# One attention layer on one core: start loads by block, forget gates by log of sigmoid, an earlier gate evacuation, and a last row tile in 512, 256, 256

## The chip, the core and the metric

The kernel runs on one core of a Trainium2 chip. The core has five engines that run beside each other and wait for each other by semaphores: TensorE (PE in the profile; its weight loads are PEld), VectorE (DVE), ScalarE (ACT), GpSimd (POOL) and SyncE (SP), which here only issues DMAs. The metric is the time of one execution on the device, in microseconds (us).

## What is computed

One layer on x of 1024 rows by 1024 columns, in fp32. A normalised and modulated input u feeds one wide projection; sixteen heads of width 64 attend over it, eight by forgetting attention (FoX) and eight by stick-breaking; an output projection and a second LayerNorm follow.

```python
mod = silu(c) @ w_ada + b_ada                       # shift, scale, gate
u = layer_norm(x) * (1.0 + scale) + shift
h = u @ w_in                                        # fq fk fv fg ff sq sk sv sg
log_f = log_sigmoid(ff + b_f)                       # 8 forget gates a row
f_cum = cumsum(log_f, axis=1)
# FoX:  softmax(q k / 8 + f_cum[q] - f_cum[k], causal) @ v
# stick-breaking:  exp(log_sigmoid(z) + sum of later log_sigmoid(-z)) @ v
y = concat(y_fox * silu(fg), y_sb * silu(sg)) @ w_out
out = layer_norm(2 ** 0.25 * x + gate * y) * ln_g + ln_b
```

## The kernel before, in words

Every fp32 operand of a matmul is split into a high part, rounded to the matmul's format, and a low part, the remainder; a product is three matmuls (high by high, low by high, high by low) into one PSUM tile. A u block is 128 of the 1024 columns of u, transposed; its parts are `uh` and `ul`, its number is kb, 0 to 7.

**The start (lines 627 to 747).** While rows 0 to 511 of u are made, block by block, five projections (START, line 570: q, k and the gate of pair 0, q and k of pair 1) are accumulated from each block as it appears. For a block kb:

- SyncE loads its modulation weights (`load_ss`, `wss`, 1 MB) and its projection weights (`load_w4`, `raws`, 256 KB for four projections; the fifth projection has two loads of its own, `load_w1`, each for four blocks). SyncE's queue is in program order, and it is written out by hand. `wss` has three buffers, so the load of block kb+3 waits until block kb's reductions are done.
- VectorE makes scale and shift with two reductions (`mod_part`, line 230, which ends with a short read into `modc`).
- TensorE transposes the block of x into the one PSUM tile `xT_early` (`u_turn`), ScalarE writes `uh` and the full value (`u_round`, lines 248 and 249, in the tile `xT_early`), and VectorE writes the remainder `ul` (`u_rest`, line 261).
- ScalarE rounds the block's weights and GpSimd makes their remainder (`start_split`, lines 608 and 609; tiles `whi_stk`, `hw` and, for the fifth projection, `whi_sth`).
- TensorE multiplies (`start_steps`, lines 622 and 625).

Step kb of the loop at line 682 multiplies block kb and prepares block kb+1. In the kernel before, the split of block 4 is issued at step 3 together with block 5's, behind block 4's rounding; blocks 4 and 5, and 6 and 7, come with one load of 512 KB each; and the two `wss` of blocks 6 and 7 come whole.

**The passage to rows 512 to 1023 (lines 736 to 838).** Row tiles 4 to 7 of x are loaded last. VectorE makes their statistics (lines 197, 198 and 189), GpSimd the inverse deviation (lines 191, 192 and 211), and ScalarE (tiles 4 and 5) or VectorE (6 and 7, line 217) normalises. Meanwhile TensorE makes v for rows 0 to 511 (`v_first`, lines 354 to 356), with a copy by ScalarE and a remainder by VectorE for each half of a tile (lines 362 and 363). Then `late_round(kb)` transposes and rounds block kb for rows 512 to 1023. PSUM tiles named T have two buffers: the tile `v_0_1` of the second `v_first` has one, the late block 0 the other, and late block 1 takes the buffer of `v_0_1` once VectorE has read it for the last time. The tiles named acc have two buffers as well: `st_g0b`, the gate of pair 0 for rows 512 to 1023, takes the buffer of `st_g0`, which `evac_g` (lines 289 and 290: tanh on ScalarE, then a multiply on VectorE) has to release.

**The forget gates (`gen_forget`, line 383)** run once, beside the stick-breaking units of pairs 2 and 3, when fillers reach them. With a = |ff|, log sigmoid is min(ff, 0) - ln(1 + exp(-a)): ScalarE does Exp and then Ln, each with a function table that has to be loaded first, and goes back to Sigmoid for the attention.

**The end (`o_half`, line 921).** Row tiles of 128 rows run through the output projection in 512-column groups, and each group adds the residual (line 934) and takes statistics (line 935). The last row tile has three groups, 512, 320 and 192 columns, 24 matmuls each. When its last group is done, the mean and inverse deviation follow, then `(r - mean) * ln_g` for each group (line 942), then the scaling and `ln_b`: by VectorE for 512 and 192 columns (line 946), by ScalarE and GpSimd for 320 (lines 958 and 959), and three DMAs write the row tile.

The order of instructions on TensorE and SyncE in the start is that of the program; on the other engines a list scheduler chooses it, within `after(...)`, which puts an instruction behind another.

Of the kernel before, what the change touches and what calls it, by code (L numbers as in the profile page):

```python
# [27 lines left out]
def tile_hybrid_layer(  # L28
# [122 lines left out]

    def load_ss(kb):
        t = sb.tile([P, 2, D], F32, tag="v", bufs=3, name=f"wss_{kb}")
        for a in ((0, 1), (1, 2)) if kb < 6 else ((0, 2),):
            nc.sync.dma_start(t[:, a[0]:a[1], :], w_ss[kb, :, a[0]:a[1], :])
        wss_sb.append(t)

    bss_sb = cp.tile([P, NB, 2], F32, tag="bss", name="bss_sb")
# [127 lines left out]

    def evac_g(p, ch, acc, sg):
        s = slice(ch * 512, ch * 512 + 512)
        nc.scalar.activation(sg[:, s], acc, AF.Tanh, scale=0.5)
        nc.vector.scalar_tensor_tensor(sg[:, s], sg[:, s], 1.0, acc, op0=ALU.add, op1=ALU.mult)  # L290

    def m_step(acc, tiles, kt, ch):
        hi, lo = tiles[kt // 4]
# [19 lines left out]
    def evac_m(p, m, ch, acc, heads=(0, 1)):  # L313
        if m == 0:
            evac_q(p, ch, acc, qst[p], heads)
        elif m == 1:
            return evac_k(p, ch, acc, kst[p], klo[p], heads)
        else:
            evac_g(p, ch, acc, sgt[p])

    def gen_m(p, m):
        tiles = fetch_m(p, m)
# [60 lines left out]
    def gen_forget():  # L383
        ff = fsb.rearrange("p h t -> p (h t)")
        ab = cp.tile([P, 64], F32, tag="fab", name="fab")
        lf = flf[:, 1:]
        nc.vector.scalar_tensor_tensor(ab, ff, -1.0, ff, op0=ALU.mult, op1=ALU.max)
        nc.scalar.activation(ab, ab, AF.Exp, scale=-1.0)
        nc.scalar.activation(ab, ab, AF.Ln, bias=1.0)
        for _ in range(FLOG):  # L390
            yield
        with after(*lows):
            nc.vector.scalar_tensor_tensor(lf, ff, 0.0, ab, op0=ALU.min, op1=ALU.subtract)

        pre = ff
        nc.vector.tensor_tensor_scan(pre, flf[:, 0:64], later.rearrange("p h t -> p (h t)"), initial=0.0,
                                     op0=ALU.add, op1=ALU.mult)
        for _ in range(FROW):
            yield
        scratch = att_tile("fscratch")  # L400
        tri, fr = scratch[:, :P], scratch[:64, P:2 * P]
        nc.gpsimd.memset(tri, 1.0)
        nc.gpsimd.affine_select(out=tri, in_=tri, pattern=[[1, P]], base=0,
                                channel_multiplier=-1, compare_op=ALU.is_ge, fill=0.0)
        fp = t_tile("fcum")[:, :64]
        nc.tensor.matmul(fp, tri, lf, start=True, stop=False)
        nc.tensor.matmul(fp, ones.to_broadcast([P, P]), pre, start=False, stop=True)
        fc = cp.tile([P, 64], F32, tag="fab", name="fc")
        nc.scalar.activation(fc, fp, AF.Copy, scale=-1.0)
        yield  # L410
        yield
        ft = t_tile("frow")[:64, :P]
        nc.tensor.transpose(ft, fc, ident)
        nc.scalar.copy(fr, ft)
        nc.sync.dma_start(f_dr.rearrange("h (t p) -> (h t) p", p=P), fr)
        yield
# [174 lines left out]
    def load_w1(h, raw=None):  # L591
        raw = start_raw(1) if raw is None else raw
        nc.sync.dma_start(raw, w_qkg[START[NW][0], START[NW][1], h])
        raw_w["h", h] = raw.rearrange("p (m c) -> p m c", m=4)
# [40 lines left out]
    load_w4(2)  # L635
    load_ss(3)
    load_w4(3)
    load_w1(1)
    for t in range(4):
        norm_stats(t)  # L640
        if t:
# [13 lines left out]
    with after(rounded):  # L655
        start_split(("k", 1))
    load_ss(4)
    load_w4(4, 2)
    for p in range(2):
        make_q(p)  # L660
        make_k(p)
# [20 lines left out]
    for kb in range(NB):  # L682
        last = kb == NB - 1
        if last:
            start_steps(ALL[:2], acc0, kb)
            for n in range(2):
                evac_m(*START[n], 0, acc0[n])
            start_steps(ALL[2:], acc0, kb)
            break
        start_steps(ALL[:4], acc0, kb, parts=(0,))  # L690
        if kb == 0:
            u_turn(2, tp=xt_early)
        elif kb > 1:
            u_turn(kb + 1, tp=xt_early)
        with after(*split_at["k", kb + 1][:1] if kb < 2 else ()):
            rounded = u_split(kb + 1) if kb == 0 else u_round(kb + 1)
        if kb == 0:
            with after(rounded):
                start_split(("h", 0))
            mod_terms(2)  # L700
        else:
            parts = range(2 if kb + 2 < NB else 0)
            late = kb in (3, 4)
            mod_terms(kb + 2, () if late else parts[:1])
            rest = in_turn(u_rest, kb + 1)
            mod_terms(kb + 2, parts if late else parts[1:])
        if kb == 0:
            start_steps(ALL[:4], acc0, kb, parts=(1,))
        elif kb == 1:
            start_steps(ALL[:4], acc0, kb, parts=(1,))  # L710
            for k in range(2):
                start_steps(ALL[4:], acc0, k)
        else:
            start_steps(ALL[4:], acc0, kb, parts=(0,))
            start_steps(ALL, acc0, kb, parts=(1,))
        if kb == 2:
            start_split(("h", 1))
        elif kb < 2:
            start_split(("k", kb + 2))
        elif kb + 2 < NB:  # L720
            with after(rounded):
                for k in ((4, 5) if kb == 3 else (kb + 2,)):
                    start_split(("k", k))
        if kb + 5 < NB:
            load_ss(kb + 5)
            if kb == 0:
                load_w4(6, 2)
        if kb == 2:
            for n in range(2):
                v0_load(n)  # L730
            load_x(4)
            for n in range(2, 4):
                v0_load(n)
            for t in range(5, NB):
                load_x(t)
        if kb == 5:
            with after(*split_at["k", NB - 1]):
                for n in range(4):
                    v0_split(n)
            norm_stats(4)  # L740
            norm_stats(5)
            norm_x(4)
        if kb == 6:
            with after(rest):
                for t in (6, 7):
                    norm_stats(t)
            make_v(0)
# [57 lines left out]
        load_gate(kt)  # L805
    v_first(2, late_acc[:, 1, :])
    with after(*late_round(0)):
        evac_m(*START[2], 0, acc0[2])
    rounded = late_round(1)
    v_first(3, acc_tile("v_0_3"))  # L810

    acc1 = [late_acc[:, 0, :], late_acc[:, 1, :], acc_tile("st_g0b")]
# [86 lines left out]
    OUT_ORDER = (6, 7, 4, 5, 2, 3, 0, 1)  # L899

    def groups(t):
        return ((0, 512), (512, 832), (832, 1024)) if t == OUT_ORDER[-1] else ((0, 512), (512, 1024))

    def o_step(t, h, pr):
        if pr == 0:
# [15 lines left out]
    def o_half(t, h):  # L921
        ts_ = slice(t * P, (t + 1) * P)
        s = slice(*groups(t)[h])
        ng = len(groups(t))
        if h == 0:
            xr = big("k", 4, f"xr_{t}")
            nc.sync.dma_start(xr, x[ts_, :])
            res[t] = (att_tile(f"r_{t}"), xr, sb.tile([P, 3, 6], F32, tag="st", bufs=3, name=f"st_b{t}")[:, :ng, :])
        r, xr, st = res[t]
        last = t == OUT_ORDER[-1]  # L930

        acc = o_acc[t, h][:, :s.stop - s.start]
        to = acc if last else r[:, s]
        nc.vector.scalar_tensor_tensor(to, xr[:, s], ALPHA, acc, op0=ALU.mult, op1=ALU.add)
        nc.vector.bn_stats(st[:, h, :], to)
        if h == ng - 1:
            mv, rs = ln_finish(st, f"b{t}")
            cuts = [slice(*g) for g in groups(t)]
            mid = [o_acc[t, j][:, :c.stop - c.start] if last else r[:, c] for j, c in enumerate(cuts)]

            def first(j):
                nc.vector.scalar_tensor_tensor(mid[j], mid[j], mv[:, 0:1], lgb[0][:, 0, cuts[j]],
                                               op0=ALU.subtract, op1=ALU.mult)

            def second(j):
                nc.vector.scalar_tensor_tensor(r[:, cuts[j]], mid[j], rs[:, 0:1], lgb[0][:, 1, cuts[j]],
                                               op0=ALU.mult, op1=ALU.add)
                (nc.scalar if j == 2 else nc.sync).dma_start(out[ts_, cuts[j]], r[:, cuts[j]])

            if not last:  # L950
                for j in range(2):
                    first(j)
                    second(j)
                return
            for j in (1, 0, 2):
                first(j)
            c = cuts[1]
            nc.scalar.activation(r[:, c], mid[1], AF.Copy, scale=rs[:, 0:1])
            nc.gpsimd.tensor_tensor(r[:, c], r[:, c], lgb[0][:, 1, c], op=ALU.add)
            nc.sync.dma_start(out[ts_, c], r[:, c])  # L960
            for j in (0, 2):
                second(j)

    def gen_out_first(t):
        for h in range(2):
# [203 lines left out]
```

## Time and profile before

| what | value |
|---|---|
| median of 3 runs | 683.64 us (683.54 to 684.12) |
| the profiled execution | 684.15 us, its span 682.44 us |
| granted TensorE clock | 0.998 |
| TensorE busy | 671.7 us (98%), 3713 matmuls |
| VectorE, ScalarE, GpSimd busy | 485.0, 380.7, 404.9 us |
| DMA, mean over the span | 119 GB/s |

The span runs from the first to the last instruction of one profiled execution; the rest of that execution's time, 1.7 us, lies around it. In the rows of a timeline stand the start in us from the span's start, the duration in us, the engine, the line, the operation, the tiles written and read, the shape, how many neighbours were merged, and in brackets how long the engine had been idle and what released it. Ends of matmuls are modelled, so for TensorE the distance between starts says more than the durations.

### The profile page before, as it was taken

To read this page: it belongs to the slowest core of one execution; us is meant where nothing else is said; L and a number is where in the kernel's file an instruction comes from. 1 tells how busy PE (TensorE), PEld (TensorE's weight loads), DVE (VectorE), ACT (ScalarE), POOL (GpSimd) and SP (SyncE) were. 2 spreads that over 40 slices of the span, in tenths; PEclk is the share of its full clock that TensorE was granted. 3 is DMA by queue.
4 is the path that set the end of the run, shared out by engine and by line. 5 is a ranking of instruction groups with operands and counts; after the bars stand their busy time and mean duration, and the time that the engine had idled before them with its cause. 6 is when DMAs were issued, how large, how long until landed. Compare 5 with 4: busy or idle time off the path is not lost.

```text
span 682.4 us, 11191 instructions
## 1 busy us (share of the span) xinstructions
PE 671.7 (98%) x3713; PEld 572.5 (84%) x3713; DVE 485.0 (71%) x996; ACT 380.7 (56%) x857; POOL 404.9 (59%) x529
## 2 busy tenths in 40 slices
PE   8999999999999999999999999999999999999995
PEld 5788898888997888889988888889988888888885
DVE  6696779868666777777676675766676777875645
ACT  5567377756567666666665564656565766521000
POOL 5550179756447656566369778786785365655411
PEclk9999999999999999999999999999999999999999
DMA  9973422112102122122034455363352297153301
GB/s 327 408 271 143 147 74 79 30 37 60 32 10 70 41 54 56 39 54 55 27 114 144 147 162 155 109 182 127 118 172 64 65 343 309 58 179 103 119 32 61
DMA packets 45272, 81.54 MB, mean 119 GB/s; under 512 B 5216, under 2 KB 19360, under 8 KB 44960
## 3 DMA queue, kind: packets, MB, share of 16 engines
q1 hardware_dynamic: 43632, 76.54, 34.4%
q10 hardware_dynamic: 1584, 4.31, 1.9%
q8 instruction: 29, 0.48, 0.3%
q14 instruction: 27, 0.22, 0.1%
HBM read 60.34 MB, written 16.29 MB: 112 GB/s over the span
## 4 chain that ended last, share of the span: by engine, by line
PE 95%; ACT 2%; DVE 2%; POOL 1%; issue 0%; DVEq 0%; POOLq 0%
PE m L296 10%; PE m L297 10%; PE m L298 10%; PE pv L530 10%; PE T L513 9%; PE S L462 5%; PE S L461 5%; PE o L917 4%; PE o L916 4%; PE o L915 4%; PE v L354 4%; PE v L356 4%; PE v L355 4%; PE st_q L622 1%; PE st_late L622 1%; PE st_k L622 1%
## 5 line engine op out<-in xcount | busy, mean ns | idle before, releaser
L516 DVE TENSOR_TENSOR pt<-T,pt 128x512 fp32r<-128x512 f32 (+2 forms) x192 | 102.6, 553 | 43.5 <-ACT pt L515 41.9
L515 ACT CAST pt<-T 128x512 fp32r<-128x512 f32 (+2 forms) x192 | 88.6, 478 | 64.5 <-PE T L513 62.6
L296 PE MATMUL m<-uh,whi 128*128 128x512 f32 x304 | 123.5, 406 | 0.0
L298 PE MATMUL m<-uh,wlo 128*128 128x512 f32 x304 | 119.9, 394 | 0.0
L297 PE MATMUL m<-ul,whi 128*128 128x512 f32 x304 | 119.8, 394 | 0.0
L496 POOL TENSOR_TENSOR be<-be,kp 128x127 f32<-128x127 f32 (+3 forms) x64 | 78.9, 1233 | 37.8 <-DVE kp L494 26.2
L490 DVE TENSOR_TENSOR_SCAN kp<-kp,floor 128x512 f32<-128x512 f32 (+2 forms) x64 | 65.0, 1016 | 25.5 <-ACT kp L483 24.2
L530 PE MATMUL pv<-pt,v 128*128 128x512 f32 x320 | 82.9, 389 | 0.0
L477 POOL TENSOR_SCALAR a<-a,l 128x1024 f32<-128x1024 f32 (+3 forms) x64 | 48.3, 754 | 36.0 <-DVE l L475 25.3
L461 PE MATMUL S<-k,q 128*128 128x512 f32 (+5 forms) x192 | 68.9, 360 | 0.3 <-ACT be L485 0.3
L298 PEld LDWEIGHTS m<-uh,wlo 128*128 128x128 f32 x304 | 57.2, 188 | 13.6
L474 ACT ACTIVATE a<-a,nm 128x1024 f32<-128x1024 f32 (+3 forms) x64 | 49.8, 778 | 29.2 <-DVE nm L469 28.9
L296 PEld LDWEIGHTS m<-uh,whi 128*128 128x128 f32 x304 | 57.3, 188 | 10.0 <-PE T L513 0.3
L462 PE MATMUL S<-kl,qz 128*128 128x512 f32 (+5 forms) x192 | 65.4, 342 | 0.0
L297 PEld LDWEIGHTS m<-ul,whi 128*128 128x128 f32 x304 | 57.4, 189 | 9.0
L530 PEld LDWEIGHTS pv<-pt,v 128*128 128x128 f32 x320 | 55.5, 189 | 9.0
L546 POOL TENSOR_TENSOR ty<-ty,sg 64x256 f32<-64x256 f32 x64 | 46.9, 732 | 23.9 <-issue 10.9
L469 DVE CUSTOM_DVE_ANT_0 a<-S,fb 128x1024 f32<-128x1024 f32 (+3 forms) x64 | 48.2, 754 | 16.6 <-PE S L462 11.7
L435 ACT CAST qz<-q 64x128 fp32r<-64x128 f32 x128 | 37.3, 296 | 33.6 <-PE S L462 32.4
L354 PE MATMUL v<-whi_v,uh 128*128 128x256 f32 (+1 forms) x192 | 54.8, 285 | 0.0
L356 PE MATMUL v<-wlo_v,uh 128*128 128x256 f32 (+1 forms) x192 | 54.3, 283 | 0.0
L483 ACT ACTIVATE kp<-S 128x128 f32<-128x128 f32 (+3 forms) x64 | 42.0, 657 | 21.8 <-PE S L462 20.5
(290 smaller groups left out, 1624.6 us busy)
## 6 DMA issues: line engine op xcount, KB each, us to landing
raw<-in_w_qkg_dram SPq DMA_DIRECT2D x38, 256.0 KB, 2.7
wss<-in_w_ss_dram SPq DMA_DIRECT2D x12, 512.0 KB, 8.6
x<-in_x_dram SPq DMA_DIRECT2D x8, 512.0 KB, 7.3
k<-k SPq DMA_DIRECT2D x32, 128.0 KB, 2.3
wg<-in_w_gate_dram SPq DMA_DIRECT2D x8, 512.0 KB, 4.5
raw_o<-in_w_out_dram SPq DMA_DIRECT2D x16, 256.0 KB, 3.0
fb<-f_dr ACTq DMA_DIRECT2D x8, 512.0 KB, 4.4
wo_dr<-whi_o SPq DMA_DIRECT2D x16, 256.0 KB, 2.0
```

The costliest lines, as they stand in the source:

```text
L296: nc.tensor.matmul(acc, hi[:, c], u_hi[kt][:, s], start=(kt == 0), stop=False)
L297: nc.tensor.matmul(acc, hi[:, c], u_lo[kt][:, s], start=False, stop=False)
L298: nc.tensor.matmul(acc, lo[:, c], u_hi[kt][:, s], start=False, stop=(kt == NB - 1))
L354: nc.tensor.matmul(acc[:, :n], u_hi[kt][:, ts_], hi[:, s], start=(kt == 0), stop=False)
L356: nc.tensor.matmul(acc[:, :n], u_hi[kt][:, ts_], lo[:, s], start=False, stop=(kt == NB - 1))
L461: nc.tensor.matmul(S[:, s, :w], qst[p][h][:, qs], kst[p][h][:, ks], start=True, stop=False)
L462: nc.tensor.matmul(S[:, s, :w], z, klo[p][:, ks], start=False, stop=True)
L490: last_dve = nc.vector.tensor_tensor_scan(rv, rv, floor[:, :ke - lo], initial=0.0, op0=ALU.mult, op1=ALU.max)
L496: nc.gpsimd.tensor_tensor(be[:, :ke - 1], be[:, :ke - 1], kp[:, 1:ke], op=ALU.mult)
L515: nc.scalar.copy(hi[:, :n, qo:qo + P], t3)
L516: lows[:] = [nc.vector.tensor_tensor(lo[:, :n, qo:qo + P], t3, hi.bitcast(F32)[:, :n, qo:qo + P], op=ALU.subtract)]
L530: nc.tensor.matmul(acc2[:, :, q0:], vt[p][:, kb, h * P:(h + 1) * P], pt[:, :, q0:], start=(kb == 0), stop=(kb == last))
```

## The change

Four parts of the program are edited.

- **Loads by block.** `load_w4` loads one block each, right behind its block's `wss`, which always comes in two halves. The second load of the fifth projection (`load_w1(1)`) moves from behind block 3's weights to behind block 4's. The split of block 4 moves to step 2, that of the fifth projection's second half to step 3, ahead of block 5's. At step 4 the first reduction for block 6 is put ahead of the remainder of block 5.
- **Forget gates.** The two ScalarE functions become Sigmoid of a and Ln of that, and the subtraction an addition: min(ff, 0) + ln(sigmoid(a)).
- **Gate evacuation.** Late block 1 is transposed as before, but its rounding now comes behind the tanh of the gate's evacuation; before it came ahead of it.
- **The last row tile.** Its groups are 512, 256 and 256 columns. ScalarE and GpSimd take 256 and then 96 columns, VectorE 512 and 160, and two DMAs write 512 columns each, the first from ScalarE's queue.

```diff
     def load_ss(kb):
...
-        for a in ((0, 1), (1, 2)) if kb < 6 else ((0, 2),):
-            nc.sync.dma_start(t[:, a[0]:a[1], :], w_ss[kb, :, a[0]:a[1], :])
+        for i in range(2):
+            nc.sync.dma_start(t[:, i, :], w_ss[kb, :, i, :])
...
-        nc.scalar.activation(ab, ab, AF.Exp, scale=-1.0)
-        nc.scalar.activation(ab, ab, AF.Ln, bias=1.0)
+        nc.scalar.activation(ab, ab, AF.Sigmoid)
+        nc.scalar.activation(ab, ab, AF.Ln)
...
-            nc.vector.scalar_tensor_tensor(lf, ff, 0.0, ab, op0=ALU.min, op1=ALU.subtract)
+            nc.vector.scalar_tensor_tensor(lf, ff, 0.0, ab, op0=ALU.min, op1=ALU.add)
...
     load_w4(3)
-    load_w1(1)
...
     load_ss(4)
-    load_w4(4, 2)
+    load_w4(4)
+    load_w1(1)
...
-            late = kb in (3, 4)
+            late = kb == 3
             mod_terms(kb + 2, () if late else parts[:1])
             rest = in_turn(u_rest, kb + 1)
             mod_terms(kb + 2, parts if late else parts[1:])
...
-        if kb == 2:
-            start_split(("h", 1))
-        elif kb < 2:
+        if kb < 2:
             start_split(("k", kb + 2))
         elif kb + 2 < NB:
             with after(rounded):
-                for k in ((4, 5) if kb == 3 else (kb + 2,)):
-                    start_split(("k", k))
+                if kb == 3:
+                    start_split(("h", 1))
+                start_split(("k", kb + 2))
         if kb + 5 < NB:
             load_ss(kb + 5)
-            if kb == 0:
-                load_w4(6, 2)
+            load_w4(kb + 5)
...
     with after(*late_round(0)):
-        evac_m(*START[2], 0, acc0[2])
-    rounded = late_round(1)
+        gated = evac_m(*START[2], 0, acc0[2])
+    with after(gated):
+        rounded = late_round(1)
...
-        return ((0, 512), (512, 832), (832, 1024)) if t == OUT_ORDER[-1] else ((0, 512), (512, 1024))
+        return ((0, 512), (512, 768), (768, 1024)) if t == OUT_ORDER[-1] else ((0, 512), (512, 1024))
...
+            def shared(c, m):
+                nc.scalar.activation(r[:, c], m, AF.Copy, scale=rs[:, 0:1])
+                nc.gpsimd.tensor_tensor(r[:, c], r[:, c], lgb[0][:, 1, c], op=ALU.add)
...
+            shared(cuts[1], mid[1])
+            c = cuts[2]
+            cut = c.stop - 96
+            shared(slice(cut, c.stop), mid[2][:, cut - c.start:])
+            second(cuts[0], mid[0])
+            second(slice(c.start, cut), mid[2][:, :cut - c.start])
+            nc.scalar.dma_start(out[ts_, cuts[0]], r[:, cuts[0]])
+            rest = slice(cuts[1].start, c.stop)
+            nc.sync.dma_start(out[ts_, rest], r[:, rest])
```

(`evac_g` and `evac_m` now return the tanh, so that `after(gated)` can name it.)

The edits move instructions at three places. The first is ScalarE at steps 2 to 4 of the start loop, from the rounding of block 3 to that of block 5. `uh_3` to `uh_5` are the rounded blocks, `hw_34` and `hw_56` hold the split weights of blocks 3 and 4, and 5 and 6, `whi_sth1` those of the fifth projection's second half. Before:

```order
L248 ACTIVATE uh_3_127<-xT_early_147,modc_140 128x512
L249 ACTIVATE xT_early_147<-xT_early_147,modc_140 128x512
L248 ACTIVATE uh_4_128<-xT_early_147,modc_140 128x512
L249 ACTIVATE xT_early_147<-xT_early_147,modc_140 128x512
L608 CAST hw_34_323<-raws_3_250 128x512
L608 CAST hw_56_398<-raws_3_250 128x512
L248 ACTIVATE uh_5_129<-xT_early_147,modc_140 128x512
```

The same stretch after:

```order
L249 ACTIVATE xT_early_147<-xT_early_147,modc_140 128x512
L609 CAST hw_34_322<-raws_2_175 128x512
L248 ACTIVATE uh_4_128<-xT_early_147,modc_140 128x512
L249 ACTIVATE xT_early_147<-xT_early_147,modc_140 128x512
L609 CAST whi_sth1_398<-raws_3_250 128x512
L609 CAST hw_56_402<-raws_3_250 128x512
L248 ACTIVATE uh_5_129<-xT_early_147,modc_140 128x512
```

Block 4's weights (`hw_34`) are now rounded ahead of `uh_4`, and the cast of the fifth projection's second half, which stood ahead of `uh_3`, has taken the free place ahead of block 5's.

The second place is VectorE where the start ends: the remainder of block 7 (`ul_7`) and the statistics of row tiles 4 and 5 (`st_a4`, `mv_a4`, `st_a5`). Before:

```order
L230 ISA wss_7_356,modc_140<-sc_all_111,wss_7_356,bss_sb_99 128x1024
L230 ISA modc_140 128x1
L197 BN_STATS st_a4_462<-x_4_362 128x6
L198 BN_STATS st_a4_462<-x_4_362 128x6
L189 BN_AGGR mv_a4_465<-st_a4_462 128x2
L261 TENSOR_TENSOR ul_7_139<-xT_early_147,uh_7_131 128x512
L197 BN_STATS st_a5_471<-x_5_367 128x6
```

The same after:

```order
L230 ISA wss_7_356,modc_140<-sc_all_111,wss_7_356,bss_sb_99 128x1024
L230 ISA modc_140 128x1
L261 TENSOR_TENSOR ul_7_139<-xT_early_147,uh_7_131 128x512
L197 BN_STATS st_a4_466<-x_4_364 128x6
L198 BN_STATS st_a4_466<-x_4_364 128x6
L189 BN_AGGR mv_a4_469<-st_a4_466 128x2
L271 SCALAR_TENSOR_TENSOR q_0_0_252<-st_q0_148,q_0_0_252 64x512
```

The remainder of block 7 has moved ahead of the statistics of row tile 4; no edit asks for that, the scheduler chose it.

The third place is ScalarE in the passage: the rounding of late blocks 0 and 1 (`uh_0`, `uh_1`), the tanh of the gate (`sg_0`) and copies of v. Before:

```order
L248 ACTIVATE uh_0_124<-xT_0_512_644,modc_140 128x512
L249 ACTIVATE xT_0_512_644<-xT_0_512_644,modc_140 128x512
L362 CAST v_1_520<-st_late_547 128x2x64
L248 ACTIVATE uh_1_125<-xT_1_512_654,modc_140 128x512
L249 ACTIVATE xT_1_512_654<-xT_1_512_654,modc_140 128x512
L289 ACTIVATE sg_0_546<-st_g0_150 128x512
```

The same after:

```order
L248 ACTIVATE uh_0_124<-xT_0_512_648,modc_140 128x512
L249 ACTIVATE xT_0_512_648<-xT_0_512_648,modc_140 128x512
L363 CAST v_1_524<-st_late_551 128x2x64
L289 ACTIVATE sg_0_550<-st_g0_150 128x512
L248 ACTIVATE uh_1_125<-xT_1_512_658,modc_140 128x512
L249 ACTIVATE xT_1_512_658<-xT_1_512_658,modc_140 128x512
```

The tanh stands ahead of late block 1's two activations, which move back by one instruction; VectorE's multiply of the gate moves ahead of late block 1's remainder in the same way.

More of the change, by code (lines that the diff above doesn't have):

```diff
@@ L288, in evac_g @@
         s = slice(ch * 512, ch * 512 + 512)
-        nc.scalar.activation(sg[:, s], acc, AF.Tanh, scale=0.5)
+        first = nc.scalar.activation(sg[:, s], acc, AF.Tanh, scale=0.5)
         nc.vector.scalar_tensor_tensor(sg[:, s], sg[:, s], 1.0, acc, op0=ALU.add, op1=ALU.mult)
+        return first
     def m_step(acc, tiles, kt, ch):
@@ L318, in evac_m @@
         else:
-            evac_g(p, ch, acc, sgt[p])
+            return evac_g(p, ch, acc, sgt[p])
     def gen_m(p, m):
@@ L943, in first, with second @@
                                                op0=ALU.subtract, op1=ALU.mult)
[L945 to L948, printed above, removed]
+            def second(c, m):
+                nc.vector.scalar_tensor_tensor(r[:, c], m, rs[:, 0:1], lgb[0][:, 1, c], op0=ALU.mult, op1=ALU.add)
+            def shared(c, m):
+                nc.scalar.activation(r[:, c], m, AF.Copy, scale=rs[:, 0:1])
+                nc.gpsimd.tensor_tensor(r[:, c], r[:, c], lgb[0][:, 1, c], op=ALU.add)
             if not last:
@@ L952, in o_half @@
                     first(j)
-                    second(j)
+                    second(cuts[j], mid[j])
+                    nc.sync.dma_start(out[ts_, cuts[j]], r[:, cuts[j]])
                 return
@@ L956, in o_half @@
                 first(j)
[L957 to L962, printed above, removed]
+            shared(cuts[1], mid[1])
[7 more added lines that the diff above has]
+            nc.sync.dma_start(out[ts_, rest], r[:, rest])
     def gen_out_first(t):
```

## The prediction

> **What bounds the kernel now.** The table of engines comes first, then TensorE's waits, then the timeline around each.
>
> ```profile
> PE 671.7 (98%) x3713; PEld 572.5 (84%) x3713; DVE 485.0 (71%) x996; ACT 380.7 (56%) x857; POOL 404.9 (59%) x529
> ...
> PE st_q L622 <- ACT hw L608: 0.4, 1, 0.4
> PE T L513 <- POOL wlo L127: 0.3, 1, 0.3
> PE S L461 <- ACT be L485: 0.3, 1, 0.3
> PE st_q L622 <- POOL hw L609: 0.2, 1, 0.2
> ```
>
> TensorE is busy 98% of the span, so an edit gains only where it shortens TensorE's own work, removes one of its few waits, or shortens what follows its last matmul. The columns of the waits are total us, times and the longest. The first and the last are TensorE waiting for block 4's weights, rounded by ScalarE and with the remainder by GpSimd. Their full price is read from the starts of matmuls:
>
> ```profile
> 29.68 0.39 PE L625 MATMUL st_k<-ul,whi_sth 128*128 128x512 f32 x1
> 30.49 0.50 PE L622 MATMUL st_q<-uh,hw 128*128 128x512 f32 x1 [0.42 <-ACT hw L608]
> ...
> 31.06 0.40 PE L622 MATMUL st_g<-uh,hw 128*128 128x512 f32 x1
> 31.29 0.40 PE L622 MATMUL st_q<-uh,hw 128*128 128x512 f32 x1
> 31.86 0.50 PE L622 MATMUL st_q<-uh,hw 128*128 128x512 f32 x1 [0.17 <-POOL hw L609]
> ...
> 59.17 0.71 PE L622 MATMUL st_late<-uh,whi_stk 128*128 128x512 f32 x2
> 60.03 0.50 PE L622 MATMUL st_g0b<-uh,whi_stk 128*128 128x512 f32 x1 [0.15 <-DVE sg L290]
> ```
>
> Starts of 512-column matmuls in a full pipeline are 0.23 apart (31.06 to 31.29). From 29.68 to 30.49 are 0.81, so 0.58 is lost; from 31.29 to 31.86 are 0.57, 0.34 lost. The matmul behind a wait lasts 0.50 in place of 0.39, another 0.11 each time. From 59.17 to 60.03 are 0.86 for two matmuls: 0.46, a start of 0.11 behind transposes, and 0.29 lost; with the restart behind it 0.40. So the removable time is 0.58 + 0.34 + 0.22 = 1.14 in the start and 0.4 in the passage.
>
> **Loads by block.** ScalarE rounded block 4's weights behind `uh_4`, with the next in one merged row:
>
> ```profile
> 28.49 0.78 ACT L248 ACTIVATE uh<-xT_early,modc 128x512 fp32r<-128x512 f32 x1 [2.50 <-PE xT_early L242]
> ...
> 29.83 1.14 ACT L608 CAST hw<-raws 128x512 fp32r<-128x512 f32 x2
> ```
>
> Ahead of `uh_4` ScalarE idled 2.50 us, from 25.99. Block 4's cast of 0.57 (half of 1.14) goes there if its weights have come by 27.9. Loads took this long, and SyncE issued them here:
>
> ```profile
> raws<-in_w_qkg_dram SPq DMA_DIRECT2D x6, 256.0 KB, 8.2
> ...
> raws<-in_w_qkg_dram SPq DMA_DIRECT2D x2, 512.0 KB, 9.3
> ```
>
> ```profile
> 16.71 1.51 SPq L155 DMA_DIRECT2D wss<-in_w_ss_dram  x2
> ...
> 22.40 0.38 SPq L587 DMA_DIRECT2D raws<-in_w_qkg_dram  x1
> ```
>
> With the fifth projection's load gone from ahead of them, block 4's weights take about the place in which the second `wss` half stood, which ended at 18.22: issued near 17.9, landed at 26.1 to 27.2. Both stalls of block 4 go: −1.14. Block 5's weights take the place at 22.40 and land at 30.6 to 31.7; they are rounded behind `uh_4`, in the idle time ahead of `uh_5`. Next could be late: `uh_5` itself, and then the reductions.
>
> ```profile
> 32.95 0.08 DVE L230 DVE_READ_ACCUMULATOR2_ANT modc<- 128x1 f32 x1
> ...
> 34.98 0.69 DVE L261 TENSOR_TENSOR ul<-xT_early,uh 128x512 fp32r<-128x512 f32 x1 [1.95 <-ACT xT_early L249]
> ```
>
> ```profile
> 33.53 0.78 ACT L248 ACTIVATE uh<-xT_early,modc 128x512 fp32r<-128x512 f32 x1 [2.57 <-PE xT_early L242]
> ```
>
> `modc` of block 5 is ready at 33.03, so `uh_5` can come 0.40 to 0.50 earlier, not 1.14, and ends near 33.9. TensorE, which took it at 34.97, would want it at 33.83:
>
> ```profile
> 34.97 0.39 PE L622 MATMUL st_q<-uh,hw 128*128 128x512 f32 x1
> ```
>
> So a tenth of the 1.14 may stay. The first reduction of block 6 now fills the 1.95 that VectorE idled ahead of 34.98, so `modc` is earlier for `uh_6` by more than TensorE is. About 1.05 of gain reaches the end of the start loop.
>
> There the order moves what nobody asked for. The remainder of block 7 stood behind the statistics of row tile 4:
>
> ```profile
> 41.43 0.69 DVE L197 BATCH_NORM_STATS2 st_a<-x 128x6 f32<-128x512 f32 x1
> ...
> 43.07 0.69 DVE L261 TENSOR_TENSOR ul<-xT_early,uh 128x512 fp32r<-128x512 f32 x1
> ...
> 54.34 0.29 DVE L363 TENSOR_TENSOR v<-v,v 128x128 fp32r<-128x128 f32 x1 [0.33 <-ACT v L362]
> ```
>
> ```profile
> 42.29 0.74 ACT L249 ACTIVATE xT_early<-xT_early,modc 128x512 f32<-128x512 f32 x1
> ...
> 55.09 1.03 PE L242 MATMUL xT<-ident,x 128*128 128x128 f32 x8
> ```
>
> The statistics took 1.64 (41.43 to 43.07), while ScalarE wrote the block's value (42.29 to 43.03). Afterwards the value comes at 43.03 − 1.1 = 41.9; VectorE does the remainder at 41.95 and the statistics behind it, done at 41.95 + 0.65 + 1.64 = 44.2. Before, both were done at 43.07 + 0.65 = 43.7. VectorE's chain is thus 0.5 later, not 1.1 earlier. From there it runs through the statistics and the normalising of row tile 7 to the last remainder of `v_0_1` (54.34 + 0.29 = 54.63); its idle 0.33 ahead of that is no slack, since ScalarE's copy of the second half waits in turn for VectorE's remainder of the first. So that buffer comes free at 55.1 to 55.25 (0.5 later, or 0.6 if GpSimd's inverse deviation also slips). TensorE's eight transposes at 55.09 are late blocks 0 and 1; the second four need this buffer, at 55.09 + 0.51 = 55.6 before, slack 0.97. With a gain of 1.05 TensorE wants it at 54.55 and loses 0.55 to 0.7, with a restart of 0.11. I take 0.75: loads by block, net −1.05 + 0.75 = −0.3. The ends: −1.1 if VectorE catches up, +0.5 if it slips by another 0.8, one row tile's reading.
>
> **Forget gates.** One table load goes.
>
> ```profile
> 208.14 1.28 ACT L388 ACT_TABLE_LOAD   x1
> 211.08 0.26 ACT L388 ACTIVATE fab<-fab 128x64 f32<-128x64 f32 x1 [1.65 <-DVE fab L387]
> ```
>
> It ended at 209.42, and ScalarE then waited 1.65 for VectorE's `fab`; without it ScalarE waits longer and restarts at 211.08 all the same. Cost 0: VectorE's work is the cover, and the load in front of Ln and the return stay. The Trainium skill's "ScalarE: Activation LUTs", section "What ACT_TABLE_LOAD costs", gives about 1283 ns for a load and 1380 ns of drain around it; the row agrees on the load, and by the page's sum an exposed one would be worth 2.66 instead of 1.28.
>
> **Gate evacuation.**
>
> ```profile
> 58.55 0.62 ACT L289 ACTIVATE sg<-st_g 128x512 f32<-128x512 f32 x1
> ```
>
> The tanh starts two activations (0.74 and 0.78, less overlap 1.33) earlier, and the multiply one remainder (0.69) earlier; the stall at 60.03 goes, −0.4. Late block 1's parts come 0.6 later; its first matmuls stand behind block 0's fifteen (15 × 0.23 = 3.5), which covers that. If `v_0_1` delays it as above, the tanh isn't behind it any more.
>
> **The last row tile.** Its 48 narrow matmuls change shape; 256 columns are seen in the passage.
>
> ```profile
> 669.00 0.31 PE L915 MATMUL o<-woh,whi_y 128*128 128x320 f32 x1
> ...
> 672.53 0.25 PE L915 MATMUL o<-woh,whi_y 128*128 128x192 f32 x1
> ...
> 675.08 0.28 PE L917 MATMUL o<-wol,y7h 128*128 128x192 f32 x1
> ```
>
> ```profile
> 46.54 0.28 PE L354 MATMUL st_late<-v_home,uh 128*128 128x256 f32 x1
> ...
> 49.38 0.28 PE L354 MATMUL v<-v_home,uh 128*128 128x256 f32 x1
> ```
>
> 24 of 320 took 3.53 (0.147 each, 0.46 ns a column); 23 steps of 192 took 2.55 (0.111, 0.58 ns a column). 24 of 256 took 2.84 (0.118, 0.46 ns a column): narrow ones pay a floor. Sum 3.53 + 24 × 0.111 = 6.19 before, 48 × 0.118 = 5.68 after: −0.51. Behind the last matmul:
>
> ```profile
> 672.73 0.50 DVE L934 SCALAR_TENSOR_TENSOR o<-xr,o 128x320 f32<-128x320 f32 x1 [2.10 <-PE o L917]
> ...
> 675.39 0.36 DVE L934 SCALAR_TENSOR_TENSOR o<-xr,o 128x192 f32<-128x192 f32 x1 [1.63 <-PE o L917]
> ```
>
> 128 columns more cost 0.14, so 64 cost 0.07, for line 934 and once more for 935: +0.14. Then the scaling:
>
> ```profile
> 678.68 0.33 SPq L948 DMA_DIRECT2D out_dram<-r  x1
> 679.11 0.38 SPq L960 DMA_DIRECT2D out_dram<-r  x1
> ```
>
> Two stores in place of three carry the same bytes; the last one's inputs have less work ahead on GpSimd (352 columns against 320, but in two pieces), which I count at nothing, −0.2 to +0.3 (one issue, 0.33). The end: −0.51 + 0.14 = −0.37, say −0.4.
>
> **Sum.** −0.3 + 0 − 0.4 − 0.4 = −1.1: the profiled execution of 684.15 becomes 683.05. It stood 0.5 above the median of 683.64; the median becomes 682.5. About 0.2%, 1.37 us, is what a measurement of this kernel can tell from no change, so 682.5 counts as the same.
>
> **Rivals.**
>
> First, VectorE does not hold TensorE in the passage. For it: between 44 and 55 the scheduler also moved smaller things on VectorE, and a part of the 0.5 may be made up where the chain waits for GpSimd. Against it: VectorE has hardly an idle moment there. Then the loads keep 1.1 and the sum is −1.9: 681.7, faster.
>
> Second, the table load counts after all. The two 0.3 waits in the first fence, on `wlo` and on `be`, lie just behind the gates, at 214.2 and 215.5, where ScalarE is late by its table loads; were `fab` ready when ScalarE is (which the shortened queue might bring), ScalarE would come out up to 1.28 earlier and both waits would go with their restarts, 0.8 in all: sum −1.9, 681.7, and with the page's 2.66 no more, since TensorE has no more to get back there. Against it: `fab` comes from VectorE, whose work ahead of it is unchanged.
>
> Third, slower: loads come late. ScalarE works in order, so block 5's cast ahead of `uh_5` stops `uh_5` until its weights have come. It decides from a landing after 32.4 (`uh_5` at 33.03 less the cast's 0.57). The queue is full:
>
> ```profile
> 28.00:32.00 4.00, 3.40 (x17) 2.23 (x15) 2.34 (x6) 2.48 (x4) 1.48 (x2) 1.00 1.06 416
> ```
>
> At 416 GB/s and all DMA engines busy, a slip of 2.6 us (1.1 MB ahead of it) lands it at 35.0 and costs TensorE 2.6 less the slack of 0.2, about 2.4 with 0.8 given by the other parts: +1.6, 685.2. For it: more and smaller loads. Against it: the bytes ahead are those of before. The Trainium skill's "DMA: Bandwidth & Descriptors", section "Rules for kernel authors", asks for 1 MiB or more per DMA, which speaks against the split loads; the row's 416 GB/s came mostly with 256 and 512 KB, so by the trace nothing is lost.
>
> **How the numbers follow.** Forecast 0.52, own range 682.2 to 683.4; VectorE free 0.28; table load 0.07; late loads 0.09; anything else 0.04. Faster by over 0.2% (below 682.27) takes the table load, 0.24 of the second case and 0.06 of the forecast's lower edge: 0.37. Slower (above 685.01): 0.09 of late loads and 0.01: 0.10. The rest, 0.53, is the same. The range reaches down to the first rival with 0.3 spare, 681.4, and up by the loads' end of +0.5 (0.8 above the sum) and a little of the tail, 683.9; what lies outside is late loads, and a part of the rest.
>
> **What would show it.** Right: no wait for `hw` at blocks 4 and 5; a new wait of TensorE of 0.5 to 0.9 for `v_0_1`'s buffer at the second four transposes near 55; no wait at `st_g0b`; the wait ahead of `fab` near 2.9; 48 matmuls in 5.7 and the last L934 0.5 earlier. Wrong: TensorE crosses the passage 1.1 earlier (first rival); ScalarE's wait for `fab` stays at 1.65 and the later loads come 1.28 earlier (second); `uh_5` behind a cast that waits for a load (third); or the tail's second store issued after 679.1.

## The result and the profile after

The changed kernel takes 682.63 us (median of 18 runs, 682.23 to 683.07), the kernel before 683.64: a ratio of 0.9984 with a 95% interval of 0.9977 to 0.9992. It is 1.0 us faster, where 1.1 was forecast. That is less than the 1.37 us which the prediction counted as no change, though the interval leaves out 1. A second set of runs gave 682.62 and 0.9985 (0.9976 to 0.9994).

The profiled execution took 682.39 us. First its engines and TensorE's waits, in the columns of before:

```profile
PE 670.2 (98%) x3713; PEld 571.7 (84%) x3713; DVE 484.8 (71%) x996; ACT 380.1 (56%) x857; POOL 406.1 (60%) x530
```

```profile
PE st_late L355 <- DVE v L364: 0.5, 1, 0.5
PE st_q L623 <- ACT uh L255: 0.3, 1, 0.3
PE T L514 <- POOL wlo L127: 0.3, 1, 0.3
PE S L462 <- ACT be L486: 0.3, 1, 0.3
```

The two waits for `hw` and the one for `st_g0b` are gone. The two behind the forget gates stand unchanged. One is new: TensorE waits for VectorE's last read of `st_late`. TensorE's timeline at the places of before, and VectorE's behind the start:

```profile
29.05 0.39 PE L626 MATMUL st_k<-ul,whi_sth 128*128 128x512 f32 x1
29.28 0.39 PE L623 MATMUL st_q<-uh,hw 128*128 128x512 f32 x1
...
50.37 0.28 PE L357 MATMUL v<-v_w,uh 128*128 128x256 f32 x1
51.15 0.39 PE L355 MATMUL st_late<-v_home,uh 128*128 128x256 f32 x1 [0.50 <-DVE v L364]
...
58.17 0.71 PE L623 MATMUL st_late<-uh,whi_stk 128*128 128x512 f32 x2
58.72 0.47 PE L623 MATMUL st_g0b<-uh,whi_stk 128*128 128x512 f32 x1
```

```profile
41.33 0.69 DVE L261 TENSOR_TENSOR ul<-xT_early,uh 128x512 fp32r<-128x512 f32 x1 [2.04 <-ACT xT_early L249]
41.94 0.69 DVE L197 BATCH_NORM_STATS2 st_a<-x 128x6 f32<-128x512 f32 x1
42.54 0.68 DVE L198 BATCH_NORM_STATS2 st_a<-x 128x6 f32<-128x512 f32 x1
43.32 0.21 DVE L189 BATCH_NORM_AGGREGATE mv_a<-st_a 128x2 f32<-128x12 f32 x1
...
50.80 0.29 DVE L364 TENSOR_TENSOR v<-st_late,v 128x128 fp32r<-128x128 f32 x1
```

Block 4's matmuls now follow at 0.23 without a gap (29.05 to 29.28). ScalarE rounds the weights of blocks 4 and 5 as soon as each has landed:

```profile
25.83 0.62 ACT L609 CAST hw<-raws 128x512 fp32r<-128x512 f32 x1 [0.48 <-DMA raws<-in_w_qkg_dram]
...
30.91 0.62 ACT L609 CAST hw<-raws 128x512 fp32r<-128x512 f32 x1 [1.09 <-DMA raws<-in_w_qkg_dram]
```

From 50.37 to 51.15 are 0.78 where a step of 256 columns is 0.12: 0.66 lost, and the next start 0.1 late. `st_g0b` comes 0.55 behind its pair, before 0.86. VectorE idled 2.04 ahead of block 7's remainder, with the statistics behind it.

Matmuls stand in the same order up to the last row tile, so the start of one in each trace gives the account:

| place | before | after | difference | step |
|---|---|---|---|---|
| first `st_q` of block 0 | 14.22 | 13.67 | −0.55 | |
| first L626 of block 0 | 19.54 | 18.91 | −0.63 | −0.08 |
| second low matmul of block 4 | 32.20 | 30.44 | −1.76 | −1.13 |
| first v tile | 46.54 | 44.79 | −1.75 | +0.01 |
| late blocks' transposes | 55.09 | 54.09 | −1.00 | +0.75 |
| second pair of `st_late` | 60.37 | 59.02 | −1.35 | −0.35 |
| last matmul | 675.08 | 673.21 | −1.87 | −0.52 |
| span | 682.44 | 680.6 | −1.84 | +0.03 |

The first 0.63 is not put down to the change. Of it 0.55 is there at the first `st_q`, ahead of which nothing is edited; this instruction starts anywhere from 13.56 to 14.63 in the profiled executions of this study. The next 0.08 is less than the 0.12 by which a kernel below with the start of before (the statistics behind block 7's remainder) moves between the same two rows. The kernel before was drawn late there, which fits that its profiled execution stood 0.5 above its median. Without the 0.63 the traces differ by 1.2, the medians by 1.0.

The end, VectorE and the stores, in the changed kernel:

```profile
667.64 0.28 PE L915 MATMUL o<-woh,whi_y 128*128 128x256 f32 x1
...
673.21 0.28 PE L917 MATMUL o<-wol,y7h 128*128 128x256 f32 x1
```

```profile
673.52 0.43 DVE L934 SCALAR_TENSOR_TENSOR o<-xr,o 128x256 f32<-128x256 f32 x1 [1.94 <-PE o L917]
673.99 0.43 DVE L935 BATCH_NORM_STATS2 st_b<-o 128x6 f32<-128x256 f32 x1
674.46 0.24 DVE L189 BATCH_NORM_AGGREGATE mv_b<-st_b 128x2 f32<-128x18 f32 x1
```

```profile
677.33 0.33 SPq L968 DMA_DIRECT2D out_dram<-r  x1
```

47 steps take 5.57, so the 48 matmuls 5.69, before 6.19. Lines 934 and 935 take 0.94 up to the aggregate (673.52 to 674.46).

### The profile page after: what moved, and what is told of

Its sections match the earlier page's. It is cut to its first block, busy times and chain, and to the rows that moved or that the text cites. A ratio compares the mean times of both kernels' runs of the same rounds, so it can differ in the third digit from the quotient of the medians.

```text
span 680.6 us, 11191 instructions
## 1 busy us (share of the span) xinstructions
PE 670.2 (98%) x3713; PEld 571.7 (84%) x3713; DVE 484.8 (71%) x996; ACT 380.1 (56%) x857; POOL 406.1 (60%) x530
## 4 chain that ended last, share of the span: by engine, by line
PE 94%; DVE 2%; ACT 1%; POOL 1%; issue 0%; POOLq 0%; DVEq 0%
PE m L297 10%; PE m L298 10%; PE m L299 10%; PE pv L531 10%; PE T L514 9%; PE S L463 5%; PE S L462 5%; PE o L917 4%; PE o L915 4%; PE o L916 4%; PE v L355 4%; PE v L357 4%; PE v L356 4%; PE st_late L623 1%; PE st_q L623 1%; PE sc_all L176 1%
```

## The experiments

Each kernel ran beside the kernel before on the same chip; the text on record stands ahead of each result.

**The four parts alone**, each on the kernel before.

> The loads by block alone, the rest as in the kernel before. My theory: 1.1 us of TensorE's waits go in the start and about 0.75 comes back where VectorE releases the PSUM tile st_late, because the remainder of block 7 now stands ahead of row tile 4's statistics; net -0.35, 683.3 us, and in the trace a wait of 0.4 to 0.7 at the third v tile near 51. Rival: the passage wait comes from the gate's evacuation, or only from all parts together; then it is missing here and the time is 682.5.

All edits of the part on loads by block are in it; the core of them:

```diff
-            nc.sync.dma_start(t[:, a[0]:a[1], :], w_ss[kb, :, a[0]:a[1], :])
+            nc.sync.dma_start(t[:, i, :], w_ss[kb, :, i, :])
...
-                load_w4(6, 2)
+            load_w4(kb + 5)
```

683.25 us against 683.79, 0.9993 (0.9984 to 1.0002). TensorE's timeline:

```profile
50.52 0.28 PE L356 MATMUL v<-v_w,uh 128*128 128x256 f32 x1
51.28 0.39 PE L354 MATMUL st_late<-v_home,uh 128*128 128x256 f32 x1 [0.49 <-DVE v L363]
```

The wait (0.64 lost) is here with the loads alone. From 17.83 on, TensorE's lead over before grows from 0.50 to 1.60, falls to 0.84 at the wait and ends at 0.96: net −0.46.

Which edit of this part removes block 4's wait was not tried apart. In the kernel before, the 512 KB load that holds block 4's weights was issued at 19.15 and landed 8.5 later, near 27.6, while ScalarE idled until 28.49. A cast of 0.62 put there would have ended near 28.3, ahead of `uh_4`. By this estimate from the rows of before, the earlier place in ScalarE's order may be enough for block 4 without the smaller loads.

> The forget gates alone. My theory: ScalarE's wait ahead of the first activation grows from 1.65 to about 2.93 us and it goes on at the same moment; 0, 683.6 us. Rival (the load counts): the waits of TensorE behind the gates shrink, -0.8, 682.8.

```diff
-        nc.scalar.activation(ab, ab, AF.Exp, scale=-1.0)
-        nc.scalar.activation(ab, ab, AF.Ln, bias=1.0)
+        nc.scalar.activation(ab, ab, AF.Sigmoid)
+        nc.scalar.activation(ab, ab, AF.Ln)
...
-            nc.vector.scalar_tensor_tensor(lf, ff, 0.0, ab, op0=ALU.min, op1=ALU.subtract)
+            nc.vector.scalar_tensor_tensor(lf, ff, 0.0, ab, op0=ALU.min, op1=ALU.add)
```

683.55 against 683.79, 0.9998 (0.9989 to 1.0007). ScalarE:

```profile
210.49 0.26 ACT L388 ACTIVATE fab<-fab 128x64 f32<-128x64 f32 x1 [2.96 <-DVE fab L387]
210.77 1.28 ACT L389 ACT_TABLE_LOAD   x1
```

The wait grew from 1.65 to 2.96, the load's 1.28 and no more, and TensorE's lead over before changes by about 0.1 at most in the whole rest of the program, with none at the two waits behind the gates. The table-load rival is out.

> The gate evacuation alone. My theory: the one wait of TensorE at st_g0b goes, -0.35 to -0.4, 683.3 us; late block 1 comes later on ScalarE by one tanh without a wait. Rival: the late block is late for TensorE in turn and the time stays 683.6.

```diff
-        evac_m(*START[2], 0, acc0[2])
-    rounded = late_round(1)
+        gated = evac_m(*START[2], 0, acc0[2])
+    with after(gated):
+        rounded = late_round(1)
```

683.43 against 683.79, 0.9995 (0.9986 to 1.0004). The wait at `st_g0b` is gone, 0.33 gained there. Later 0.31 is given back, in two steps near 548 and 555; at the first, the kernel before and the changed one lose 0.21, this one 0.39:

```profile
547.81 0.47 PE L297 MATMUL m<-uh,whi 128*128 128x512 f32 x1 [0.22 <-DVE kl L284]
```

The same two steps come back in one other kernel below (the late loads). Why they come and go was not tried.

> The last row tile alone. My theory: the 48 narrow matmuls of the last row tile take 5.7 in place of 6.2 us, VectorE's part behind them 0.14 more, and the end comes 0.35 to 0.4 earlier, 683.3 us. Rival: the larger second store ends later by what TensorE won, 683.6.

```diff
-        return ((0, 512), (512, 832), (832, 1024)) if t == OUT_ORDER[-1] else ((0, 512), (512, 1024))
+        return ((0, 512), (512, 768), (768, 1024)) if t == OUT_ORDER[-1] else ((0, 512), (512, 1024))
...
+            shared(cuts[1], mid[1])
...
+            nc.scalar.dma_start(out[ts_, cuts[0]], r[:, cuts[0]])
+            rest = slice(cuts[1].start, c.stop)
+            nc.sync.dma_start(out[ts_, rest], r[:, rest])
```

683.17 against 683.79, 0.9994 (0.9985 to 1.0003). TensorE gains 0.50 over the 48 matmuls, and the last issue comes at 678.29 in place of 679.11, of which 0.40 is this execution's earlier start: −0.42 for the tail. The larger second store takes nothing back.

None of the four is told from no change by its time alone. Their ratios add up to −0.0020, the whole is −0.0016 (and −0.0015 again); it is the traces that place the parts.

**The passage: whose fault is the wait?**

> The kernel before, with nothing changed but that the statistics of row tiles 4 and 5 come behind block 7's remainder. My theory (VectorE's order there makes the passage wait): VectorE's chain is late by up to 1.6 us, TensorE waits 0.4 to 0.5 at the third v tile where it waited for nothing, 684.1 us. Rival (the wait comes from the later loads of x): no wait, 683.6.

```diff
-            norm_stats(4)
-            norm_stats(5)
-            norm_x(4)
         if kb == 6:
+            with after(rest):
+                norm_stats(4)
+                norm_stats(5)
+            norm_x(4)
```

684.43 against 683.85, 1.0008 (0.9999 to 1.0017): 0.6 slower by the medians, which the interval does not tell from no change. The trace tells it: the order alone brings the wait to the kernel before, whose loads are untouched. VectorE, then TensorE:

```profile
42.46 0.69 DVE L261 TENSOR_TENSOR ul<-xT_early,uh 128x512 fp32r<-128x512 f32 x1 [1.55 <-ACT xT_early L249]
43.07 0.69 DVE L197 BATCH_NORM_STATS2 st_a<-x 128x6 f32<-128x512 f32 x1
...
51.83 0.29 DVE L363 TENSOR_TENSOR v<-st_late,v 128x128 fp32r<-128x128 f32 x1 [0.22 <-ACT v L362]
```

```profile
51.51 0.28 PE L356 MATMUL v<-v_w,uh 128*128 128x256 f32 x1
52.18 0.39 PE L354 MATMUL st_late<-v_home,uh 128*128 128x256 f32 x1 [0.40 <-DVE v L363]
```

The 1.55 that VectorE now idles is the room the statistics had, and TensorE loses 0.55 and 0.1.

> The changed kernel, with row tile 4's statistics put ahead of block 7's remainder as in the kernel before. My theory: the statistics fill the 2.04 us that VectorE idled ahead of that remainder, its chain is about 0.9 earlier, the wait of 0.66 near 51 goes with its restart, 681.9 us. Rival (row tiles 4 to 7 land too late, being loaded behind more separate loads): VectorE waits for row tile 4 instead, block 7's remainder comes late too, and the time stays at 682.6 or goes to 683.

```diff
-        nc.vector.bn_stats(st[:, 1, :], src[:, 512:1024])
+        taken[0] = nc.vector.bn_stats(st[:, 1, :], src[:, 512:1024])
...
-            norm_stats(4)
+            with after(*turn_of):
+                norm_stats(4)
+            turn_of.append(taken[0])
```

682.06 against 683.85, 0.9974 (0.9964 to 0.9985); against the changed kernel (682.63) 0.57 less by the medians, with intervals that overlap. VectorE, then TensorE:

```profile
40.29 0.69 DVE L197 BATCH_NORM_STATS2 st_a<-x 128x6 f32<-128x512 f32 x1 [0.30 <-DMA x<-in_x_dram]
40.90 0.68 DVE L198 BATCH_NORM_STATS2 st_a<-x 128x6 f32<-128x512 f32 x1
42.04 0.69 DVE L261 TENSOR_TENSOR ul<-xT_early,uh 128x512 fp32r<-128x512 f32 x1 [0.46 <-ACT xT_early L249]
```

```profile
51.08 0.28 PE L357 MATMUL v<-v_w,uh 128*128 128x256 f32 x1
51.31 0.38 PE L355 MATMUL st_late<-v_home,uh 128*128 128x256 f32 x1
```

Row tile 4 had landed 0.3 after VectorE was free, and its statistics fit ahead of the remainder, which waits for ScalarE as before. The new wait is gone but for 0.2: 51.08 to 51.31 are 0.23 for a step of 0.12, and the next start is 0.1 late. Both halves of the theory stand: the order makes the wait, and undoing it returns most of the gain. The later issue of the x loads is not the cause.

**The late-loads rival, priced.**

> The changed kernel, with the weights of blocks 5, 6 and 7 each one place later in SyncE's queue, block 5's behind 1 MB more. It prices the late-loads rival. At 410 GB/s 1 MB is 2.5 us; block 5's cast waited for its load until 30.91 and would end at 34.0, ScalarE's rounding of block 5 stood at 32.50: TensorE is held about 1.5 us, 684.1 us. If the queue has slack that the trace doesn't show, 682.6.

```diff
-            load_w4(kb + 5)
+            if kb:
+                load_w4(kb + 4)
+            if kb == 2:
+                load_w4(7)
```

684.69 against 683.85, 1.0012 (1.0003 to 1.0022); 2.06 above the changed kernel, where 1.5 was expected. TensorE and ScalarE:

```profile
33.02 0.39 PE L626 MATMUL st_k<-ul,whi_sth 128*128 128x512 f32 x1
34.56 0.50 PE L623 MATMUL st_q<-uh,hw 128*128 128x512 f32 x1 [1.15 <-ACT hw L609]
```

```profile
32.55 0.78 ACT L248 ACTIVATE uh<-xT_early,modc 128x512 fp32r<-128x512 f32 x1 [2.69 <-DVE modc L230]
...
33.89 0.62 ACT L609 CAST hw<-raws 128x512 fp32r<-128x512 f32 x1
```

Block 5's weights were issued at 24.71 and landed 8.5 later, near 33.2; in the changed kernel they had come by 30.91. The scheduler put the cast behind `uh_5`, so the form of the stall is that of the kernel before: a wait for the high part, another for the low, and the pair again for block 6. By the starts TensorE falls 2.7 behind the changed kernel up to block 6, and gets 0.77 back in the passage: being later, it doesn't wait for VectorE there. So here too, as with the order of VectorE, time lost or won ahead of the passage is settled against VectorE's chain. The rest up to 2.3 in this trace are the two late steps of the gate evacuation's run.

**The table loads, from the other side.**

> The changed kernel with the logarithm left out of the forget gates (a copy in its place), so that the two table loads that are not covered by a wait, in front of Ln and on the way back, are gone: 2.56 us of ScalarE. My theory: TensorE has lost 0.9 us just behind the gates and gets back at most that and its restarts, -1.0, 681.6 us. If a load also costs its drain, ScalarE is more than 2.6 earlier, up to 5.3, seen between the gate's activations and the next ones; TensorE has no more to get back. If ScalarE is not what TensorE waits for there, 682.6.

```diff
-        nc.scalar.activation(ab, ab, AF.Ln)
+        nc.scalar.activation(ab, ab, AF.Copy)
```

682.14 against 683.85, 0.9972 (0.9961 to 0.9984); 0.5 below the changed kernel by the medians, 0.8 by the ratios of the two to the kernel before, 1.02 by the two waits in the traces (212.89 and 214.22 in the changed kernel; the leads there grow by 0.49 and 0.53). ScalarE here, then in the changed kernel:

```profile
210.00 0.26 ACT L389 ACTIVATE fab<-fab 128x64 f32<-128x64 f32 x1 [2.96 <-DVE fab L388]
...
211.29 0.29 ACT L484 ACTIVATE kp<-S 128x128 f32<-128x128 f32 x1
```

```profile
209.72 0.26 ACT L389 ACTIVATE fab<-fab 128x64 f32<-128x64 f32 x1 [2.97 <-DVE fab L388]
209.99 1.28 ACT L390 ACT_TABLE_LOAD   x1
...
212.42 1.28 ACT L484 ACT_TABLE_LOAD   x1
213.72 0.28 ACT L484 ACTIVATE kp<-S 128x128 f32<-128x128 f32 x1
```

From `fab` to the first `kp` it is 1.29 here and 4.00 there: two loads cost 2.71, their own 2.56 and 0.15. So a load that is not covered does reach TensorE, and the one that the change removes was the one that is covered.

**A better version**, in three steps from the kernel with the statistics first.

> The kernel with row tile 4's statistics ahead of block 7's remainder, and besides the first reduction for block 5 ahead of block 4's remainder, where VectorE idled 2.03 us. My theory: the wait for block 5's rounding (0.12 and its restart, near 33) goes too, another -0.2 against the kernel with the statistics alone (682.06), 681.85 us. Rival: the first half of block 5's modulation weights lands after 28.2, VectorE waits for it with block 4's remainder behind it, and TensorE is late by up to 0.5: 682.5.

```diff
-            late = kb == 3
+            late = False
```

681.89 against 683.78, 0.9972 (0.9962 to 0.9982). The wait at 33 is gone, though VectorE did wait for the load ahead of block 5's first reduction, as the rival had it:

```profile
29.05 1.28 DVE L230 CUSTOM_DVE_ANT_0 wss<-sc_all,wss,bss_sb 128x1024 f32<-128x1024 f32 x1 [1.58 <-DMA wss<-in_w_ss_dram]
```

It landed in time all the same; 0.17 in the medians is less than they can tell.

> The kernel with both of VectorE's moves (681.89), and the logarithm of the forget gates put behind the query cast of the second stick-breaking unit that follows, where ScalarE idled 0.61 and 1.89 us. My theory: the table loads lie in those idle stretches, TensorE's two waits behind the gates (0.47 and 0.42 with restarts, 1.0) go, and a late T cast and a late kp cost up to 0.5 in their place: 681.2 us. Rival: what waits for the cast and for kp is as tight as before, the two waits only move by two units: 681.9.

```diff
-        nc.scalar.activation(ab, ab, AF.Ln)
-        for _ in range(FLOG):
+        for _ in range(16):
             yield
+        with after(query[0]):
+            nc.scalar.activation(ab, ab, AF.Ln)
...
-        for _ in range(FROW):
+        for _ in range(FROW + FLOG - 16):
```

(`query[0]` is the last query cast.) 681.88 against 683.68, 0.9972 (0.9962 to 0.9982): nothing gained, as the rival had it, but not where it had it. The two waits are gone; 0.2 is lost near 220.9, and a new wait stands at the sum of the gates:

```profile
225.98 0.40 PE L299 MATMUL m<-uh,wlo 128*128 128x512 f32 x1
226.81 0.43 PE L408 MATMUL fcum<-flf,fscratch 128*128 128x64 f32 x2 [0.43 <-POOL be L499]
```

GpSimd's triangle of ones for that sum was made at 226.19, behind a product for the next unit.

> The kernel with the later logarithm, and GpSimd's triangle for the sum of the forget gates made 8 fillers earlier, in the 2.73 us that GpSimd idled ahead of 220.90. In the kernel without it (681.88) TensorE's two waits behind the gates were gone, but fcum waited 0.6 for that triangle, with its restart 0.7. My theory: that wait goes too, 681.2 us. Rival: something else holds the sum, VectorE's scan for one, or the units are late in turn, 681.9.

```diff
+        nc.gpsimd.memset(tri, 1.0)
+        nc.gpsimd.affine_select(out=tri, in_=tri, pattern=[[1, P]], base=0,
+                                channel_multiplier=-1, compare_op=ALU.is_ge, fill=0.0)
         for _ in range(FROW + FLOG - 16):
             yield
...
-        nc.gpsimd.memset(tri, 1.0)
-        nc.gpsimd.affine_select(out=tri, in_=tri, pattern=[[1, P]], base=0,
-                                channel_multiplier=-1, compare_op=ALU.is_ge, fill=0.0)
```

681.28 against 683.67, 0.9963 (0.9950 to 0.9977). It beats both kernels, the changed one by 1.3 us by the medians. Its table of TensorE's waits ends with the start:

```profile
PE sc_all L176 <- POOL ident masks.py:199: 1.6, 1, 1.6
PE st_q L624 <- ACT uh L255: 0.5, 1, 0.5
PE xT_early L242 <- ACT x L218: 0.3, 1, 0.3
```

The changed kernel, run beside the version with the later logarithm:

> The changed kernel again, on the same chip as the kernel with the later logarithm, so that the two are compared directly. 682.6 us, about 0.8 above my theory for that kernel's two other moves (681.9).

682.62 us, 0.74 above that version.

## Why the prediction held, and where it did not

Two rows of the kernel before that the prediction did not weigh, the last remainder of `v_0_0` on VectorE and TensorE's next use of its tile:

```profile
51.40 0.29 DVE L363 TENSOR_TENSOR v<-st_late,v 128x128 fp32r<-128x128 f32 x1 [0.21 <-ACT v L362]
```

```profile
52.23 0.28 PE L354 MATMUL st_late<-v_home,uh 128*128 128x256 f32 x1
```

Point by point:

- **Start, −1.05.** Measured −1.13 up to block 4 and the same at the first v tile; between them 0.23 was lost at block 5, where `uh_5` waited for `modc`, and as much came back near 39. Block 4's cast waited for its load until 25.83 and block 5's until 30.91. With the 0.63 by which this execution ran early put back, these are 26.5 and 31.5, both within the landings forecast (26.1 to 27.2, 30.6 to 31.7).
- **Passage, +0.75.** The size was right (+0.75), the place and the working were not. The step that failed is "the second four need this buffer": I took the tile `v_0_1` as the first thing that VectorE's chain holds, with a slack of 0.97, and passed over the tile before it on the same chain, `v_0_0` in `st_late`. Its last remainder ended at 51.69 before (51.40 + 0.29) and TensorE used the tile again at 52.23: 0.54 of slack, the smaller one. Held there, TensorE didn't wait for `v_0_1` any more. And the chain's slip was too large: 0.5 later at the statistics was right (43.53 and the start's 0.63, 44.2), but by 50.80 it had been made up, 51.43 with the 0.63 against 51.40. A chain that is no later is late enough when its customer comes 1.1 earlier. A slip too large against a slack too large gave the right sum, by luck.
- **Forget gates, 0.** As worked out: a wait of 2.97, near 2.9 forecast. The rival had both waits behind the gates shrink; they stayed at 0.3. Its price for them, 0.8, was low: they gave back 1.02 when the logarithm was left out.
- **Gate evacuation, −0.4.** −0.35, and late block 1 waited for nothing.
- **Last row tile, −0.37.** 48 matmuls in 5.69 (5.68 forecast); lines 934 and 935 0.94 in place of 0.80, the 0.14 forecast; the last issue 679.11 to 677.33, which is −1.78 with −1.36 brought along from before the tail: −0.42.
- **Rivals.** That VectorE doesn't hold TensorE fell with the wait at 51.15; with the order mended the kernel came to 682.06, most of the way to that rival's 681.7. Late loads didn't happen; made to happen, they cost 2.1 by another way than the one forecast, and the mechanism (ScalarE stopped at a cast ahead of `uh_5`) was not seen. The prediction's price for them was not worked out rightly either: 2.6 later than the landing it forecast, 30.6 to 31.7, is 33.2 to 34.3 and not 35.0, so its own sum gives at most +0.9 in place of +1.6.

The forecast of 682.5 missed by 0.1, well inside what the first 20 us of an execution can vary.

## What to carry to other kernels

When a stage gets earlier, list every buffer that another engine's chain releases behind it, in order of the slack in the trace of before, and take the smallest, not the last. Then look at what a scheduler moved without being asked: here 0.75 of 1.1 us was lost in the passage, and putting row tile 4's statistics back into an idle stretch, ahead of block 7's remainder, returned 0.55 of it in the trace. A table load taken out of a wait was worth nothing; the two a few instructions later were worth 1 us of TensorE's time, and moving them into idle stretches paid only when GpSimd's small preparation moved too.

## What the runs showed of the hardware

- Two ScalarE table loads cost 2.71 us with all that lies around them, 1.28 each and 0.15 together. The Trainium skill's "ScalarE: Activation LUTs", section "What ACT_TABLE_LOAD costs", has the load right and adds a drain of about 1380 ns per switch, which this measurement does not show.
- Matmuls of 320 columns cost 0.147 us each, of 256 0.118, of 192 0.111: from 256 to 192 columns next to nothing is saved in this kernel.
- In windows of 4 us from 20 to 40 us the DMA engines moved 395 to 406 GB/s in the changed kernel, 404 to 416 in the kernel before, some 3% less, and the loads by block alone bring 1088 more packets under 2 KB (20448 against 19360). The prediction had it that smaller loads lose nothing. Whether their size or their order makes the 3% was not tried; no wait of TensorE in the changed kernel is one for a DMA.
- Executions whose programs are alike up to the first projection start it anywhere within 1.07 us (13.56 to 14.63). On a change of 1 us, two profiles are compared from behind that point.
